# Block-diagonal HGRN states, alternating heads, and a smaller DMA scratch in the mixers of a two-block net

## The chip, the cores and the metric

The kernel runs on one core of a Trainium2 chip. Its time is the device time of one execution in microseconds; three executions of the kernel before gave 3905.02, 3905.59 and 3907.46 us. A core has TensorE (PE, the matrix engine, whose weight loads the profile counts apart as PEld), VectorE (DVE), ScalarE (ACT), GpSimd (POOL) and the DMA queues, each with its own stream of instructions, tied together by semaphores.

## The reference

A float32 net on 512 latent tokens and 256 context tokens of width 1024. Block 1 has two layers, each with token mixers and a mixture of 16 experts. Block 2 (differential attention, forgetting attention, two feed-forward nets) follows and isn't touched. The change is in the mixers of block 1: neighbourhood attention with six heads, HGRN2 with six heads, a short convolution. The HGRN2 part runs a gated linear recurrence over the tokens, once forward and once backward, context first; the context's last state starts the latents:

```python
def step(s, xs):                      # one chunk; s is a [64, 64] state per head
    qc, kc, gc, vc = xs
    a = jnp.cumsum(gc, axis=2)
    ...
    scores = jnp.sum(qc[:, :, :, None, :] * kc[:, :, None, :, :] * decay, axis=-1)
    o = jnp.einsum('bhts,bhsv->bhtv', scores, vc) + jnp.einsum('bhtk,bhkv->bhtv', qc * jnp.exp(a), s)
    a_last = a[:, :, -1:, :]
    s_new = jnp.exp(a_last[:, :, 0, :, None]) * s + jnp.einsum('bhsk,bhsv->bhkv', kc * jnp.exp(a_last - a), vc)
    return s_new, o
```

In the neighbourhood attention each query scores a window of 256 nearby latent keys and all 256 context keys, with one softmax over both.

## The kernel before

Activations lie with channels on the partitions and tokens on the free axis. Two heads of width 64 make a pair that fills 128 partitions; so there are three head pairs for HGRN and three for the neighbourhood attention. `mixers` runs, for each pair p: five columns of the input projection (`take`), `hgrn(p)`, three more columns, `na_prepare` and `na_attention`. A tile scheduler orders the instructions of each engine by priority when the program is built: projections are marked `later`, so they fill the places at which the mixers wait. HGRN has its own thread of PSUM banks, tag "s" (four); the attention uses tag "f" (two).

Projections. A weight tile is split on ScalarE into a rounded part (`wh`, line 244) and on VectorE into the rest (`wl`, line 245), three buffers of each. TensorE multiplies three times (lines 252 to 254).

Modulation in the background. Matrix-vector products run on VectorE (line 174). Their tiles `g` have two buffers and are loaded by DMAs that GpSimd issues (line 166), in order.

HGRN of one pair (`hgrn`, lines 715 to 766). The 768 tokens are six chunks of 128. `hg_gates` gives the decays' sums. `hg_sums` forms, for two chunks g at a time, the key-value sums: four transposes (line 784), eight matmuls in which the heads alternate (line 793), one copy of 128x256 out of PSUM (line 795). Eight steps on VectorE make states from the sums (line 739), in the tile `ls`, which `hg_gates` hands back as `kv`. A state is 128x64: rows 0 to 63 hold the first head's, rows 64 to 127 the second's. Then for each two chunks, `hg_scores` makes the scores `sc` on three engines, down to 32x32 products (line 821) and copies of 32x32 diagonals (line 835). At line 760 the output is added up in PSUM, head by head and chunk by chunk: score times value (`vt`, 128x64 weights), then state times query for each direction (64x64 weights). ScalarE copies it out (line 762). Last come the sums of squares of a head's output (line 479) and what VectorE makes of them (line 482). Layer 0 puts out all six chunks, layer 1 the four of the latents. Chunks 0 and 1 have one state product a head each, the others two.

Neighbourhood attention. `scores(j)` fills, for each of four query blocks j, one bank a head: 256 window scores (line 573) and 256 context scores (line 574). `values(j)` multiplies the transposed probabilities with the values, heads alternating (line 600), and ScalarE copies the result out (line 601).

Of the kernel before, what the change touches and what calls it, by code (L numbers as in the profile page):

```python
# [17 lines left out]
D, T, TC, KD = 1024, 512, 256, 8  # L18
TA = T + TC
CHUNKS = (8, 7, 7)  # L20
NEG = -1.0e30
KSTART = (0, 8, 24, 32)
# [29 lines left out]
class Slots:  # L52
    """A pool whose tags have their own numbers of buffers."""
# [8 lines left out]
class Net:  # L62
# [16 lines left out]
    @contextmanager  # L79
    def phase(self, name, sb, ps):  # L80
        """A part of the net with its own temporaries, in SBUF and in PSUM."""
        with self.tc.tile_pool(name=name, bufs=1, reuse_waits="tile") as s, self.psum(name, ps):
            old, self.tp = getattr(self, "tp", None), Slots(s, sb)
            yield
            self.tp = old
# [11 lines left out]
    def later(self, by=LATER):  # L97
        """What gives way to everything else that is ready."""
        return self.tc.high_priority(offset=-by)
# [5 lines left out]
    def on(self, psum, small):  # L105
        """A thread of its own: its banks and its small tiles."""
# [38 lines left out]
    def cond(self, name):  # L145
        """silu of a condition on every partition, and the generator that loads it."""
        cb = self.gp.tile([128, D], F32, tag="cb", name="cb", bufs=2)
        src = self.a[name]
# [9 lines left out]
    def gemv(self, wT, tiles, targets):  # L158
        """wT: [n, 128, 1024] in DRAM; targets: list of (cond tile, dst [128, n], bias).
        A generator: each step loads a tile and computes with the one before."""  # L160
# [24 lines left out]
    def paced(self, ins, wait=False):  # L185
        """Not issued before the last product so far, or not begun before its end."""
# [4 lines left out]
    def fill(self, n):  # L191
        """n steps of the matrix-vector products in the background."""
# [13 lines left out]
    def first_mods(self):  # L206
        """Shift and scale of the first norm, latent and context, on the tensor engine. A generator, a step for
        each block of the contraction."""
# [23 lines left out]
    def split(self, src, nk):  # L232
        """The rounded part and the rest of nk blocks [128, 128]."""
# [37 lines left out]
    def newton(self, y, v):  # L271
        """y = v ** -0.5."""
# [9 lines left out]
    def inv_rms(self, st, tag=None, paced=False):  # L282
        """1 / rms of each token, tokens on the partitions: [128, blocks]."""
# [14 lines left out]
    def spread(self, y, paced=False):  # L298
        """[128, blocks] to all partitions, tokens on the free axis."""
# [14 lines left out]
    def normed(self, x, r, A, B, split=True, pool=None, tag=None):  # L314
        """(x * rstd) * A + B, as its rounded part and the rest, or whole."""
# [30 lines left out]
    def transposed(self, dst, src, n, tag=None):  # L346
        """dst[:, j, :] = src[:, 128 j:128 (j + 1)]^T for n blocks."""
# [13 lines left out]
    def project(self, w, nf, h, evac, ks=range(KD), tags="m"):  # L361
        """w: [nf/2, 128, 2*1024] packed tiles; evac(f, psum). A generator, a step for each tile."""
# [19 lines left out]
    def lower_bounds(self):  # L382
        """For each direction and layer > 0: log lb, log(1 - lb), and their difference, per channel."""
# [18 lines left out]
    def mixers(self, l, h, hc):  # L402
        """Token mixers: the mixed tokens, 8 tiles for the latents and 8 for the context."""
# [65 lines left out]
    def head_rstd(self, segs, n, tag="nt"):  # L469
        """1 / rms over each 64 partitions, for tiles [128, tokens]; one PSUM tile each."""  # L470
# [25 lines left out]
    def na_prepare(self, l, p, d, need):  # L496
        """Normed and rotated queries and keys; values with the tokens on the partitions."""
# [57 lines left out]
    def na_attention(self, l, p, d, mix, mixc, need):  # L555
# [8 lines left out]
        def scores(j):  # L564
            v = (0, 1, 1, 2)[j]
            S = []
            for e in range(2):
                es = slice(64 * e, 64 * e + 64)
                if (e, v) not in bias:
                    bias[e, v] = self.na_bias(nb, e, v)  # L570
                b = self.bank()
                qb = q[es, 128 * j:128 * j + 128]
                nc.tensor.matmul(b[:, :256], qb, k[es, :, KSTART[j]:KSTART[j] + 32], start=True, stop=True)
                nc.tensor.matmul(b[:, 256:], qb, d["nk", "o"][es], start=True, stop=True)
                S.append(b)
# [96 lines left out]
    def hg_gates(self, l, p, S):  # L672
        """S: [first logits, -, -, second logits]. Over it, for the keys k and the decays' running sums c within
        each 128 tokens: [c1 - log k1, c1, c2, c2 + log k2]; c2 leaves out the token itself. Also the sums' ends,
        and k1 + k2."""
# [38 lines left out]
        return tot, ls[:, 0], ls[:, 1]  # L714

    def hgrn(self, l, p, d, mix, mixc, need):
        """The tokens lie context first; chunks of 128."""
        nc = self.nc
        S, q = d["z"], d["hq"]
        tot, ks, kv = self.hg_gates(l, p, S)  # L720
# [11 lines left out]
        kv = kv.rearrange("p (s c m) -> p s c m", s=2, c=6)  # L732
# [8 lines left out]
        for g in range(0 if need else 1, 3):  # L741
# [7 lines left out]
            for e in range(2):  # L749
                es = slice(64 * e, 64 * e + 64)  # L750
                first = True
                for i in range(2):
                    c, cs = 2 * g + i, slice(128 * i, 128 * i + 128)
                    ops = [(vt[:, c, es], sc[:, e, i])]
                    for dr in range(2):
                        if c != orders[dr][0]:
                            before = orders[dr][orders[dr].index(c) - 1]
                            ops.append((kv[es, dr, before], qt[es, dr, cs]))
                    for lhsT, rhs in ops:
# [942 lines left out]
```

## Time and profile before

| what | value |
| --- | --- |
| median of three executions | 3905.59 us |
| span of the profiled execution, first to last instruction | 3901.2 us |
| mean granted TensorE clock | 0.963 |
| TensorE busy | 3663.6 us, 94% |
| VectorE busy | 2172.9 us, 56% |
| ScalarE busy | 1445.6 us, 37% |
| GpSimd busy | 147.8 us, 4% |

The profiler gives the span from the first to the last instruction; the median of the timed executions lies 4.4 us above it. The mixers of layer 0 run from about 75 to 520 us, those of layer 1 from about 1040 to 1420 us. The experts come between and behind, block 2 from about 1800 us on. A float32 matmul leaves two records in the trace. In a row of a timeline "x4" means four such records in a run, the first number is where it starts and the second how long until the last ends; "[0.79 <-DVE sc L835]" is idle time of the engine just before, and what ended it. Names like `t` stand for the temporaries `t1` (queries with decay, `qt`), `s`, `f` and `m` for the banks.

### The profile page before, as it was taken

To read this page: it belongs to the slowest core of one execution; us is meant where nothing else is said; L and a number is where in the kernel's file an instruction comes from. 1 tells how busy PE (TensorE), PEld (TensorE's weight loads), DVE (VectorE), ACT (ScalarE), POOL (GpSimd) and SP (SyncE) were. 2 spreads that over 40 slices of the span, in tenths; PEclk is the share of its full clock that TensorE was granted. 3 is DMA by queue.
4 is the path that set the end of the run, shared out by engine and by line. 5 is a ranking of instruction groups with operands and counts; after the bars stand their busy time and mean duration, and the time that the engine had idled before them with its cause. 6 is when DMAs were issued, how large, how long until landed. Compare 5 with 4: busy or idle time off the path is not lost. (4 is left out here: it accounts for less than half of the span.)

```text
span 3901.2 us, 54964 instructions
## 1 busy us (share of the span) xinstructions
PE 3663.6 (94%) x21248; PEld 2659.1 (68%) x21248; DVE 2172.9 (56%) x5458; ACT 1445.6 (37%) x2827; POOL 147.8 (4%) x267
## 2 busy tenths in 40 slices
PE   7999998999899997988999998999989999999998
PEld 4777785333577775535888776788868888677887
DVE  5899874122688864215566665655643334764334
ACT  4566431111456631113233454323333233553222
POOL 0000000000000000000010000001100000000000
PEclk8999998999999997999999998999989999999999
DMA  5223254876433465995555321455522222012222
GB/s 203 70 80 101 77 196 167 327 275 259 156 111 109 135 215 199 356 356 179 194 194 189 113 76 54 142 193 205 191 80 97 96 94 95 33 52 79 97 102 81
DMA packets 154197, 588.04 MB, mean 151 GB/s; under 512 B 18048, under 2 KB 57256, under 8 KB 111952
## 3 DMA queue, kind: packets, MB, share of 16 engines
q1 hardware_dynamic: 113760, 442.43, 31.5%
q0 software_dynamic: 37872, 137.90, 10.5%
q10 hardware_dynamic: 2304, 4.20, 0.3%
q8 instruction: 167, 2.74, 0.3%
q14 instruction: 94, 0.77, 0.1%
HBM read 575.01 MB, written 9.46 MB: 150 GB/s over the span
## 5 line engine op out<-in xcount | busy, mean ns | idle before, releaser
L245 DVE TENSOR_TENSOR wl<-raw,wh 128x512 fp32r<-128x512 f32 (+1 forms) x826 | 558.3, 677 | 722.4 <-ACT wh L244 712.8
L244 ACT ACTIVATE wh<-raw 128x512 fp32r<-128x512 f32 (+1 forms) x826 | 512.1, 622 | 1203.2 <-PE m L253 835.1
L252 PE MATMUL m<-h,wh 128*128 128x512 f32 x1632 | 661.3, 406 | 30.6 <-DVE t L323 8.4
L253 PE MATMUL m<-h,wh 128*128 128x512 f32 x1632 | 658.3, 404 | 6.6 <-DVE h L326 5.2
L254 PE MATMUL m<-h,wl 128*128 128x512 f32 x1632 | 658.8, 404 | 1.1 <-DVE wl L245 1.1
L174 DVE SCALAR_TENSOR_TENSOR junk<-g,cb 128x512 bf16<-128x512 f32 (+1 forms) x440 | 374.1, 850 | 29.8 <-DMA g<-in_modT 17.5
L252 PEld LDWEIGHTS m<-h,wh 128*128 128x128 f32 x1632 | 315.4, 193 | 104.5 <-ACT h L325 19.1
L253 PEld LDWEIGHTS m<-h,wh 128*128 128x128 f32 x1632 | 313.8, 192 | 81.1 <-DVE h L326 16.3
L254 PEld LDWEIGHTS m<-h,wl 128*128 128x128 f32 x1632 | 313.9, 192 | 68.7 <-issue 6.9
L254 PE MATMUL m<-e,wl 128*128 128x512 f32 x832 | 325.7, 392 | 7.9 <-DVE wl L245 7.9
L252 PE MATMUL m<-e,wh 128*128 128x512 f32 x832 | 325.3, 391 | 0.5 <-ACT wh L244 0.5
L253 PE MATMUL m<-e,wh 128*128 128x512 f32 x832 | 324.9, 391 | 0.0
L252 PE MATMUL f<-h,wh 128*128 128x512 f32 x768 | 299.5, 390 | 0.0
L254 PE MATMUL f<-h,wl 128*128 128x512 f32 x768 | 299.1, 389 | 0.0
L253 PE MATMUL f<-h,wh 128*128 128x512 f32 x768 | 299.0, 389 | 0.0
L1106 PE MATMUL m<-raw,xg 128*64 128x512 f32 (+1 forms) x1264 | 258.5, 609 | 10.5 <-DMA raw<-in_exp_gu 10.5
L254 PEld LDWEIGHTS m<-e,wl 128*128 128x128 f32 x832 | 157.0, 189 | 40.9 <-DVE wl L245 8.3
L1106 PEld LDWEIGHTS m<-raw,xg 128*64 128x64 f32 (+1 forms) x1264 | 64.1, 126 | 175.0 <-issue 147.6
L252 PEld LDWEIGHTS m<-e,wh 128*128 128x128 f32 x832 | 157.2, 189 | 33.5 <-ACT wh L244 1.3
L253 PEld LDWEIGHTS m<-e,wh 128*128 128x128 f32 x832 | 157.0, 189 | 32.7
L252 PEld LDWEIGHTS f<-h,wh 128*128 128x128 f32 x768 | 144.5, 188 | 30.1 <-PE m L253 0.2
L254 PEld LDWEIGHTS f<-h,wl 128*128 128x128 f32 x768 | 144.3, 188 | 30.3 <-DVE wl L245 0.2
(455 smaller groups left out, 5170.0 us busy)
## 6 DMA issues: line engine op xcount, KB each, us to landing
raw<-in_exp_gu SPq DMA_DIRECT2D x98, 1024.0 KB, 6.6
raw<-in_ffn_in SPq DMA_DIRECT2D x88, 1024.0 KB, 4.8
g<-in_adaT POOLq DMA_DIRECT2D x144, 512.0 KB, 3.9
raw<-in_exp_dn SPq DMA_DIRECT2D x48, 1024.0 KB, 6.7
g<-in_modT POOLq DMA_DIRECT2D x80, 512.0 KB, 3.9
raw<-in_w_in SPq DMA_DIRECT2D x30, 1024.0 KB, 4.8
raw<-in_ffn_out SPq DMA_DIRECT2D x32, 896.0 KB, 4.6
raw<-in_ffn_out SPq DMA_DIRECT2D x16, 1024.0 KB, 4.7
```

Of the source, the lines that this page charges most:

```text
L174: self.paced(nc.vector.scalar_tensor_tensor(self.junk, before[0][:, js], 1.0, cb[:, js], op0=OP.mult, op1=OP.mult, accum_out=part[:, j:j + ...
L244: self.nc.scalar.activation(hi, src, AF.Copy)
L245: self.nc.vector.tensor_tensor(lo, src, hi.bitcast(F32), op=OP.subtract)
L252: nc.tensor.matmul(out, wh[k], hh[k], start=(first and k == ks[0]), stop=False)
L253: nc.tensor.matmul(out, wh[k], hl[k], start=False, stop=False)
L254: self.last = nc.tensor.matmul(out, wl[k], hh[k], start=False, stop=(last and k == ks[-1]))
L1106: self.nc.tensor.matmul(out[es, c:c + n], xg[:, es], t, start=start, stop=stop)
```

## The change

- In `scores(j)` both heads' banks are taken first; the order is window e0, window e1, context e0, context e1, where it was window e0, context e0, window e1, context e1.
- The states get a tile of their own, `kv`, 128 x 2 directions x 6 chunks x 128. Each state is a 128x128 block with the first head's 64x64 in one corner, the second's in the opposite one, and zeros elsewhere. GpSimd zeroes the tile in each call of `hgrn`; `hg_sums` copies out of PSUM in two parts of 64 partitions; the recurrence runs over 128x128.
- The output in `hgrn` adds first the states, one matmul of 128x128 weights for both heads, 54 where there were 108, and then the 60 products of score and value, heads alternating.
- The scratch for the descriptors of DMAs that GpSimd issues is 8192 bytes a partition; it was the default.

The other hunks remove docstrings and comments. The core of the diff:

```diff
@@ scores
-            S = []
+            S = [self.bank(), self.bank()]
             for e in range(2):
-                es = slice(64 * e, 64 * e + 64)
                 if (e, v) not in bias:
                     bias[e, v] = self.na_bias(nb, e, v)
-                b = self.bank()
-                qb = q[es, 128 * j:128 * j + 128]
-                nc.tensor.matmul(b[:, :256], qb, k[es, :, KSTART[j]:KSTART[j] + 32], start=True, stop=True)
-                nc.tensor.matmul(b[:, 256:], qb, d["nk", "o"][es], start=True, stop=True)
-                S.append(b)
+            for part in range(2):
+                for e in range(2):
+                    es = slice(64 * e, 64 * e + 64)
+                    ks = d["nk", "o"][es] if part else k[es, :, KSTART[j]:KSTART[j] + 32]
+                    nc.tensor.matmul(S[e][:, 256 * part:256 * part + 256], q[es, 128 * j:128 * j + 128], ks,
+                                     start=True, stop=True)
@@ hgrn
-        kv = kv.rearrange("p (s c m) -> p s c m", s=2, c=6)
+        kv = self.tmp("kv", 2 * TA).rearrange("p (s c m) -> p s c m", s=2, c=6)
+        nc.gpsimd.memset(kv, 0.0)
         for g in range(3):
             self.hg_sums(g, S, tot, vt, kv)
...
             po = self.bank()[:, :256]
-            for e in range(2):
-                es = slice(64 * e, 64 * e + 64)
-                first = True
-                for i in range(2):
-                    c, cs = 2 * g + i, slice(128 * i, 128 * i + 128)
-                    ops = [(vt[:, c, es], sc[:, e, i])]
-                    for dr in range(2):
-                        if c != orders[dr][0]:
-                            before = orders[dr][orders[dr].index(c) - 1]
-                            ops.append((kv[es, dr, before], qt[es, dr, cs]))
-                    for lhsT, rhs in ops:
-                        nc.tensor.matmul(po[es, cs], lhsT, rhs, start=first, stop=False, skip_group_check=True)
+            first = True
+            for i in range(2):
+                c, cs = 2 * g + i, slice(128 * i, 128 * i + 128)
+                for dr in range(2):
+                    if c != orders[dr][0]:
+                        before = orders[dr][orders[dr].index(c) - 1]
+                        nc.tensor.matmul(po[:, cs], kv[:, dr, before], qt[:, dr, cs], start=first, stop=False,
+                                         skip_group_check=True)
                         first = False
+            for i in range(2):
+                for e in range(2):
+                    es, cs = slice(64 * e, 64 * e + 64), slice(128 * i, 128 * i + 128)
+                    nc.tensor.matmul(po[es, cs], vt[:, 2 * g + i, es], sc[:, e, i], start=False, stop=False,
+                                     skip_group_check=True)
@@ hg_sums
-        nc.vector.tensor_copy(kv[:, :, 2 * g:2 * g + 2], pv[:, :256].rearrange("p (s c m) -> p s c m", s=2, c=2))
+        pv = pv[:, :256].rearrange("p (s c m) -> p s c m", s=2, c=2)
+        for e in range(2):
+            es = slice(64 * e, 64 * e + 64)
+            nc.vector.tensor_copy(kv[es, :, 2 * g:2 * g + 2, es], pv[es])
@@ kernel
-    nc = bacc.Bacc("TRN2", target_bir_lowering=False, num_devices=1)
+    nc = bacc.Bacc("TRN2", target_bir_lowering=False, num_devices=1, dynamic_dma_scratch_size=8192)
```

Where the program puts these instructions follows. Lines in the changed kernel are a few numbers higher: 756 is the state product, 762 score times value, 800 the two copies, 740 the recurrence, 733 the zeroing, 826 the scores' products.

TensorE before, the output of the second two chunks of the first head pair; `sc,hvt` is score times value, `t_1046,ls` state times query.

```order
L254 MATMUL m<-h,wl 128x512
L252 MATMUL m<-c,wh 128x256
L760 MATMUL s<-sc,hvt 64x128
L760 MATMUL s<-t_1046,ls 64x128 x2
L760 MATMUL s<-sc,hvt 64x128
L760 MATMUL s<-t_1046,ls 64x128 x2
...
L821 MATMUL s<-hx 128x128 x4
L821 MATMUL s<-hx 64x64 x8
```

Both kinds of product stand together, in turns, behind the finished scores.

TensorE of the change, the third two chunks of the same pair; `t_1225,kv` is state times query, `hx` and `hq,ls` are the scores' products, `halves` sums of squares.

```order
L826 MATMUL s<-hx 32x32 x16
L756 MATMUL s<-t_1225,kv 128x128 x4
L479 MATMUL f<-halves,nt 128x2 x4
L826 MATMUL s<-hx 32x32 x16
...
L826 MATMUL s<-hx 32x32 x16
L830 MATMUL s<-hq,ls 32x32 x16
...
L254 MATMUL m<-h,wl 128x512
L762 MATMUL s<-sc,hvt 64x128 x4
L252 MATMUL m<-c,wh 128x256
```

The state products have moved ahead, to where their operands are ready, among the scores' products; only four matmuls stand behind the finished scores. Between the two places there are 24 projection matmuls of 512 columns, 15 of 256, and four groups of 16 small products.

GpSimd before, from the start; `cb` are the conditions, `g` the modulation tiles, `row` the experts' gathers.

```order
L151 DMA cb<-in_c 128x1024
L151 DMA cb<-in_c_ctx 128x1024
L166 DMA g<-in_modT 128x1024 x48
L992 DMA row<-scratch_h,idx_6624 128x1024 x2
L992 DMA row<-scratch_c,idx_6997 128x1024
```

GpSimd of the change, the same stretch.

```order
L733 MEMSET kv 128x1536
L151 DMA cb<-in_c 128x1024
L151 DMA cb<-in_c_ctx 128x1024
L166 DMA g<-in_modT 128x1024 x6
L733 MEMSET kv 128x1536
L166 DMA g<-in_modT 128x1024 x11
L733 MEMSET kv 128x1536
L166 DMA g<-in_modT 128x1024 x31
```

Three zeroings of layer 0 now stand in the queue, two of them among the loads of modulation tiles; layer 1 has three more, the first ahead of its first load, the others 12 and 11 loads further on.

VectorE of the change, the place at which the tile behind the second zeroing is first read: `hsmall<-s` is the step on the sums of squares, and the read with DMASW0 in its waits is that tile's.

```order
L177 TENSOR_TENSOR mctx_83<-part 128x1 [waits DVE_49]
L482 TENSOR_SCALAR hsmall<-s 128x12 [waits PE_49]
L280 SCALAR_TENSOR_TENSOR small<-small 128x12 [waits DVE_49]
L174 SCALAR_TENSOR_TENSOR junk,part<-g,cb 128x512 [waits DMASW0_49]
L275 TENSOR_SCALAR hsmall<-hsmall 128x12 [waits DVE_49]
L488 COPY nt<-small 128x512 [waits DVE_49]
L278 TENSOR_TENSOR hsmall<-hsmall 128x12 [waits DVE_49]
L488 COPY nt<-small 128x256
L279 SCALAR_TENSOR_TENSOR hsmall<-hsmall 128x12 [waits DVE_49]
L245 TENSOR_TENSOR wl<-raw,wh 128x512 [waits DMAHW5_49,Activation_49]
```

Before, the read of the same tile stood seven rows ahead of the step; now it stands two rows behind it.

## Rows read from the trace of the kernel before

**Rows 1.** The page: busy time of TensorE, share of the span, instructions.

```profile
PE 3663.6 (94%) x21248; PEld 2659.1 (68%) x21248; DVE 2172.9 (56%) x5458; ACT 1445.6 (37%) x2827; POOL 147.8 (4%) x267
```

**Rows 2.** Busy times in both mixer stretches: the sum row (instructions left out).

```profile
sum 825.00, PE 779.43 PEld 604.54 DVE 697.84 ACT 463.13 POOL 51.45; mean PE 389.71 PEld 302.27 DVE 348.92 ACT 231.57 POOL 25.72
```

**Rows 3.** Waits of TensorE, 75 to 520: total us, times, longest.

```profile
PE s L760 <- DVE sc L835: 5.2, 7, 1.0
```

**Rows 4.** Waits of VectorE, 75 to 520, then 1040 to 1420.

```profile
DVE wl L245 <- ACT wh L244: 15.0, 7, 5.1
...
DVE junk L174 <- DMA g<-in_modT: 13.2, 6, 3.9
```

**Rows 5.** Line 760 in the whole trace: count, min/median/max ns, first, last, forms.

```profile
L760 PE MATMUL s<-t,ls x216: 269/269/472, 128.9 to 1363.3; 64*64 64x128 f32 x108
...
L760 PE MATMUL s<-sc,hvt x120: 272/294/475, 128.6 to 1362.7; 128*64 128x128 f32 x120
```

**Rows 6.** Timeline of TensorE, first output run: start, length, what, [idle before].

```profile
128.61 0.40 PE L760 MATMUL s<-sc,hvt 128*64 128x128 f32 x2 [0.79 <-DVE sc L835]
...
131.47 0.38 PE L821 MATMUL s<-hx 64*128 64x128 f32 x2
```

**Rows 7.** The same for the second output run.

```profile
147.77 0.43 PE L760 MATMUL s<-sc,hvt 128*64 128x128 f32 x2
148.13 0.65 PE L760 MATMUL s<-t,ls 64*64 64x128 f32 x4
148.71 0.43 PE L760 MATMUL s<-sc,hvt 128*64 128x128 f32 x2
```

**Rows 8.** The same for weight loads of the first run.

```profile
128.94 0.19 PEld L760 LDWEIGHTS s<-t,ls 64*64 64x64 f32 x2 [0.17 <-issue]
```

**Rows 9.** TensorE at the neighbourhood values of one block, then the next scores.

```profile
189.67 0.39 PE L253 MATMUL m<-h,wh 128*128 128x512 f32 x1
189.90 0.40 PE L254 MATMUL m<-h,wl 128*128 128x512 f32 x1
190.23 0.66 PE L600 MATMUL f<-nt,nv 128*64 128x128 f32 x8
190.72 0.61 PE L600 MATMUL f<-nt,nvc 128*64 128x128 f32 x8
191.25 0.93 PE L573 MATMUL f<-ev,nq 64*128 64x256 f32 x3
...
192.24 0.59 PE L574 MATMUL f<-evc,nq 64*128 64x256 f32 x2
```

**Rows 10.** TensorE at four transposes of the key factors, and what follows.

```profile
106.38 0.66 PE L784 MATMUL s<-ident,t 128*128 128x128 f32 x4
106.79 0.48 PE L252 MATMUL m<-h,wh 128*128 128x512 f32 x1
```

**Rows 11.** End of the first head pair: TensorE's last output products, VectorE's next step.

```profile
168.24 0.54 PE L760 MATMUL s<-t,ls 64*64 64x128 f32 x3
...
171.74 0.17 DVE L482 TENSOR_SCALAR hsmall<-s 128x12 f32<-128x12 f32 x1 [3.23 <-PE s L479]
```

**Rows 12.** TensorE at the scores of a first block.

```profile
176.80 0.71 PE L573 MATMUL f<-ev,nq 64*128 64x256 f32 x4
177.31 0.63 PE L574 MATMUL f<-evc,nq 64*128 64x256 f32 x4
```

**Rows 13.** VectorE by line and form, 75 to 1420: count | busy us, mean ns.

```profile
L811 DVE TENSOR_TENSOR hx<-hz 128x256 f32<-128x256 f32 x105 | 44.0, 420 | 19.5 <-PE s L821 19.3
...
L739 DVE SCALAR_TENSOR_TENSOR ls<-ls,hsmall 128x64 f32<-128x64 f32 x48 | 12.2, 278 | 0.0
...
L795 DVE COPY ls<-s 128x256 f32<-128x256 f32 x18 | 7.6, 423 | 4.4 <-PE s L793 3.9
```

**Rows 14.** The chain of waits in block 2: start, length, what.

```profile
2829.63 0.47 POOL g L166
...
2836.02 1.23 DVE junk L174 x2
```

More of the change, by code (lines that the diff above doesn't have):

```diff
@@ L713, in hg_gates @@
         nc.vector.tensor_add(ls[:, 0], ls[:, 0], ls[:, 1])
-        return tot, ls[:, 0], ls[:, 1]
+        return tot, ls[:, 0]
     def hgrn(self, l, p, d, mix, mixc, need):
@@ L719, in hgrn @@
         S, q = d["z"], d["hq"]
-        tot, ks, kv = self.hg_gates(l, p, S)
+        tot, ks = self.hg_gates(l, p, S)
         m = mix[3 + p] = self.ap.tile([128, T], F32, "x", "mix")
```

2 rows, old and new, of the table ada are left out of this document.

## The prediction

> **What bounds the kernel now.** I first read the busy times of the page. TensorE works in 94% of the span [rows 1], so time taken off it is worth most where no other engine is close behind. Then the busy times of the two stretches in which the mixers run, 75 to 520 and 1040 to 1420 us, 825 us together: TensorE 779, VectorE 698, ScalarE 463 [rows 2]. The reader is to see two things: TensorE is idle for only 825 − 779 = 46 us, and VectorE, with 127 us idle, is nearer to it here than in the whole span. Next the waits of both engines. TensorE hardly waits for VectorE: the largest such row is 5.2 us, for the scores' diagonal at the output product [rows 3]. VectorE waits for ScalarE's rounded weights, 15.0 us, and for modulation tiles, 13.2 us [rows 4]. ScalarE in its turn rounds into one of three buffers that TensorE empties, so this wait is TensorE's pace passed back. The mixers are TensorE's, with VectorE next.
>
> **The output product (state and values).** All records stand under one line: 216 of the state product, in 64x64 tiles, 120 of the value product, in 128x64 tiles [rows 5]; a float32 matmul leaves two records, so these are 108 and 60 matmuls. They come in 15 runs, one for each pair of chunks. In the three runs of the context chunks, of 16 records, the two forms alternate: 131.47 − 128.61 = 2.86 us [rows 6]. In the other twelve, of 24 records, a round of two value records, 0.36, and four state records, 0.58, takes 148.71 − 147.77 = 0.94 [rows 7], and four rounds 3.76. Together 3×2.86 + 12×3.76 = 53.7 us.
> The rows show why it is so long: the weight load of each new form starts after 0.17 us in which nothing holds it but issue [rows 8], and there are eight such changes in a run.
> After: each run has 8 value records, heads alternating. The neighbourhood values are that form already: 16 records in 191.25 − 190.23 = 1.02 us [rows 9], so 8 take 0.51, and with one change of form, 0.17, it is 0.68; 15×0.68 = 10.2 us.
> The 54 full-size state products have 108 records of 128x128 with 128 columns. The nearest rows are the four transposes, each with its own load, in 106.79 − 106.38 = 0.41 us [rows 10], 0.103 a record: 11.1 us. The order puts most of them beside projections, which are of the same form; some six runs stand between two groups of 32x32 products, as the run in the second order shown, or between these and sums of squares, and cost about two changes of 0.17 each, 2.0 us. Sum 10.2 + 11.1 + 2.0 = 23.3; TensorE saves 53.7 − 23.3 = 30 us. Bounds: if a full-size record takes the 0.18 us that a value record takes in rows 7, the states cost 19.4, and the saving is 22; with no extra changes of form it is 35. I take 30, since the transposes differ from the new matmul only in that one operand is an identity.
> A rule speaks against this part. The Trainium skill, "TensorE: Matmul & The Clock Gate", section on LDWEIGHTS and the part on what overlaps, gives a load P/1.2 ns (107 for 128 columns) and lets it overlap running matmuls only where their row groups differ. By it a full-size record is load plus stream, about 0.16 us as an estimate from that page, the states cost 17.3 instead of 11.1, and the saving is 24. The trace disagrees: four transposes of this size with four loads in 0.41 us [rows 10].
>
> **The wait before it.** The state products no longer stand behind the diagonal copies, so when these end only 0.5 us of work is left in front of ScalarE's copy, where 2.9 to 3.8 us were. In six places the wait for the last sums of squares, 3.23 us in the first pair [rows 11], may fall by up to 3 us. This is the same time as above seen from VectorE, and I don't count it again.
>
> **Neighbourhood scores.** The two heads already use different halves of the rows, and in a first block they run side by side: 176.80 to 177.94, 1.14 us [rows 12]. In a third block the second head starts late and the group takes 191.25 to 192.83, 1.58 us [rows 9]. Its bank is the one that the values of an earlier block left, and that is still so: when that bank comes free decides, not the order. I cost the interleaving at 0. Bounds: if all of some 14 late groups took 1.14, −14×0.44 = −6 us; if the first head now waits with the second's bank in each, +14×0.2 = +3.
>
> **VectorE.** The state's copy of 128x256 takes 423 ns, 18 times; the two copies that replace it cover half the partitions with as many elements a partition. If the time goes with the elements of a partition, +18×423 = 7.6 us; at the least 0. I take 7.6, as 128x256 on another line takes 420 [rows 13]. The recurrence grows from 128x64, 278 ns, to 128x128, which lies between that and the 420 of 256: near 0.34, 48×0.065 = 3.1 us (bounds 0 and 6.8). VectorE rises by 10.7 to 709 us of a stretch that should shorten to some 800.
>
> **GpSimd.** The zeroing has no row. VectorE's 420 ns for a sixth of its elements [rows 13] makes 2.5 us; the bounds are 0 and that, and I take 2, as the size is what counts. It is a wait more than a cost: GpSimd's queue is in order, the zeroing waits for the last state product of the pair before, and behind it stand the loads of the modulation tiles. The seventh, which before had nothing but a free buffer to wait for, now waits for that product. From GpSimd's start to the first read of a tile the chain shows 2836.02 − 2829.63 = 6.4 us [rows 14], so the tile can be read 8.4 us after the last state product. When is it wanted? The order puts the read two rows behind the sums-of-squares step. In the old run that step comes at 171.74, 3.5 us after the start of the last products of the output at 168.24 [rows 11]. And in the new order 24 projections of 512 columns stand between the last state product and the last value products, 0.23 us each [rows 9], 5.5 us, with 15 of 256 columns and four groups of small products besides, at least 8 us together. So the read is wanted 8 + 3.5 = 11.5 us after the product, and the tile is there by 8.4. In layer 1 the held tiles are read 11 and 5 rows behind the step, in the third pair 30. I take 0 for the standing; the bounds are 0 and six times 8, 48. The halved scratch of the descriptors costs nothing: at most two tile loads are in flight.
>
> **Sum.** TensorE −30. VectorE has 10.7 us more to do, on an engine busy for 709 of some 800; TensorE has only three buffers of split weights to outlast it, and the copies and the recurrence lie in the chain of each head pair. I charge it nearly whole, +10. Net −20 on the profiled span of 3901.2, so 3881; the runs' median is 4.4 above that span, and the forecast in its terms is 3905.6 − 20 = 3886 us. Its own range: saving 22 with 14.4 charged (both upper bounds of VectorE) and 3 for the scores, 3901; saving 35 with nothing charged, 3871.
>
> **Rivals.**
> Gain swallowed: VectorE at 709 of 800 sets the pace and TensorE's 30 us become waits for split weights. For it: VectorE's 85% in these stretches. Against: its largest wait is for ScalarE's weights, which TensorE's buffers hold back. With 4 us passed on, 3902: no change.
> The zeroing holds the queue (the slower side): one place, the tile loads behind the six memsets. If every held load comes 8 us after VectorE wants it, VectorE stands for 48 us, with the split of the next weights queued behind the read, and TensorE behind that; it decides from the point at which more than 30 us of it reach TensorE, and with all of it the time is 3905.6 − 30 + 48 = 3924. For it: the order shows the memsets ahead of the loads, and VectorE already waits 13.2 us for such tiles [rows 4]. Against: the distance worked out above.
> More than forecast: the shorter tail frees banks earlier, the late score groups run side by side, −6, and only 2 us of VectorE's work show: 3905.6 − 30 − 6 + 2 = 3872.
> That the change doesn't do what it says holds for the interleaving, which I price at 0.
>
> **How the numbers follow.** A difference under 0.2% (7.8 us) can't be told from none here. Forecast 0.65, swallowed gain 0.17, slower side 0.10, more than forecast 0.08. Of the forecast's case 0.02 lies within 0.2%. Faster 0.63 + 0.08 = 0.71, same 0.17 + 0.02 = 0.19, slower 0.10. The range reaches from 3870, below the best case, to 3903, past the swallowed gain's 3902; it leaves out the slower side, and part of the swallowed gain.
>
> **What would show it.** Right: 15 value runs of 8 records near 0.5 us; state records 0.10 to 0.12 apart beside projections; TensorE's busy time in the two stretches 25 to 35 us lower; VectorE's two copies near 420 ns each; no new VectorE wait for a modulation tile over 2 us behind a memset. Wrong: full-size state records at 0.16 us or more; TensorE's waits for split weights up by 15 us or more; waits for modulation tiles of 20 us or more in all.

## The result and the profile after

The changed kernel takes 3868.8 us in the median (four runs, 3863.0 to 3874.4) against 3906.5 (four runs); the ratio is 0.9898, 95% interval 0.9885 to 0.9911. That is 38 us less, where 20 were forecast, and just outside the range. The profiled span is 3864.0 us against 3901.2.

Where the time went is seen by cutting both traces at the same projection matmuls: from the first product of line 252 in the program to the 513th (mixers of layer 0), and from the 561st to the 961st (layer 1). Before, these stretches took 502.7 and 428.8 us; now 488.4 and 402.1, together 41.0 less. The rest of the span takes 2973.6 us, where it was 2969.7; in the profiles of the experiments below, none of which changes its instructions, it lies between 2966.8 and 2983.3. So the gain lies in the mixers, and layer 1, with six of the 15 output runs, gains more than layer 0 with nine.

The busy times of the changed kernel in the two stretches; the columns are length, then TensorE, its weight loads, VectorE, ScalarE, GpSimd, the granted clock, and the DMA share and rate.

```profile
40.96:529.32 488.36, 459.57 (x4547) 364.30 (x4547) 430.94 (x1339) 259.69 (x555) 28.25 (x50) 0.96 0.30 101
1032.79:1434.88 402.09, 381.75 (x3432) 298.39 (x3431) 334.45 (x1007) 237.69 (x467) 31.91 (x57) 0.98 0.46 156
sum 890.45, PE 841.31 PEld 662.69 DVE 765.39 ACT 497.38 POOL 60.16; mean PE 420.66 PEld 331.34 DVE 382.69 ACT 248.69 POOL 30.08
```

The same two stretches before, their sum:

```profile
sum 931.48, PE 875.43 PEld 683.59 DVE 755.92 ACT 497.90 POOL 54.69; mean PE 437.71 PEld 341.79 DVE 377.96 ACT 248.95 POOL 27.34
```

So TensorE's busy time fell by 34.1 us and its idle time from 56.1 to 49.1, though VectorE is now busy for 765 of 890 us, 86% (81% before).

The new products, by line in the whole trace; they answer to [rows 5].

```profile
L756 PE MATMUL s<-t,kv x108: 275/275/377, 118.8 to 1317.7; 128*128 128x128 f32 x108
...
L762 PE MATMUL s<-sc,hvt x120: 272/273/324, 129.6 to 1331.0; 128*64 128x128 f32 x120
```

The lengths of single records say little, because records overlap; their spacing counts. TensorE's timeline in the first run, which answers to [rows 6]:

```profile
118.56 0.35 PE L826 MATMUL s<-hx 64*32 64x32 f32 x32
118.84 0.71 PE L756 MATMUL s<-t,kv 128*128 128x128 f32 x4
119.48 0.35 PE L826 MATMUL s<-hx 64*32 64x32 f32 x32
...
129.60 0.66 PE L762 MATMUL s<-sc,hvt 128*64 128x128 f32 x8
130.19 0.88 PE L826 MATMUL s<-hx 64*128 64x128 f32 x18
```

Four state records take 0.64 us, eight value records 0.59, and the states are done 10 us before the values. Added up from the first record of each run to the next instruction, the 17 runs of states take 13.7 us and the 15 of values 8.8, 22.5 where the old runs took 54.4 in the same way. The wait in front of them, TensorE's waits for the scores' diagonal in both stretches (answering to [rows 3]):

```profile
PE s L762 <- DVE sc L840: 0.9, 2, 0.5
...
PE s L762 <- DVE sc L840: 0.8, 3, 0.3
```

Before, these were 5.2 and 4.1 us. VectorE's added work by form, 75 to 1381 us, and one of its waits (answering to [rows 13]):

```profile
L800 DVE COPY kv<-s 64x256 f32<-64x256 f32 x36 | 15.2, 422 | 4.1 <-PE s L795 3.5
...
L740 DVE SCALAR_TENSOR_TENSOR kv<-kv,hsmall 128x128 f32<-128x128 f32 x48 | 14.7, 347 | 0.2
...
L816 DVE TENSOR_TENSOR hx<-hz 128x256 f32<-128x256 f32 x105 | 44.1, 422 | 2.1 <-PE s L826 1.6
```

A copy of half the partitions takes 422 ns, as long as the whole one took; the wider recurrence takes 347 ns. VectorE's wait for TensorE's products of the scores, 19.3 us before at line 811, is 1.6 us. GpSimd's zeroing, and VectorE's step on the sums of squares at the end of the first pair (answering to [rows 11]):

```profile
L733 POOL MEMSET kv<- 128x1536 f32 x6 | 8.3, 1384 | 306.5 <-DVE c L326 238.6 <-PE f L219 34.3 <-PE s L756 33.6
```

```profile
165.78 0.17 DVE L482 TENSOR_SCALAR hsmall<-s 128x12 f32<-128x12 f32 x1 [1.09 <-PE s L479]
```

This wait was 3.23 us. Over all six places it fell from 15.5 to 7.5 us.

VectorE's waits for modulation tiles, 75 to 500 us and then layer 1 (answering to [rows 4]):

```profile
DVE junk L174 <- DMA g<-in_modT: 0.2, 1, 0.2
...
DVE junk L174 <- DMA g<-in_modT: 13.8, 5, 6.9
```

The first window ends before a wait of 4.5 us at the end of the layer-0 mixers. With it layer 0 has 4.7 us, where the kernel before has 4.3, 3.2 of them at the same place.

### A third term: the clock

The work doesn't explain why the stretches of most experiments below differ. Idle time and the granted clock do. At the end of the layer-1 mixers TensorE projects the mixed tokens and runs dry while VectorE finishes the last tiles. The kernel before, in pieces of 5 us (columns as above):

```profile
1415.00:1420.00 5.00, 3.89 (x16) 2.56 (x15) 5.00 (x11) 1.02 (x2) 0.00 (x0) 1.00 1.02 410
1420.00:1425.00 5.00, 2.29 (x5) 1.50 (x6) 3.69 (x12) 1.26 (x2) 0.53 (x1) 0.60 1.05 372
1425.00:1430.00 5.00, 5.00 (x21) 4.69 (x20) 1.40 (x4) 0.63 (x1) 0.00 (x0) 0.50 1.02 420
1430.00:1435.00 5.00, 3.70 (x15) 2.96 (x14) 2.44 (x7) 0.77 (x2) 0.00 (x0) 0.50 0.64 222
```

TensorE stands for 3.07 us, and the clock goes from 1.00 to 0.50, that is from 2.4 to 1.2 GHz, and stays there for more than 10 us. The Trainium skill, "TensorE: Matmul & The Clock Gate", "What's actually happening", says that idleness throttles the array to half the clock and that activity releases it. The trace agrees with the first half, with the four rows above; of the release they show nothing, as in the third TensorE is busy for all 5 us and the clock stays at 0.50.

The changed kernel at the same work, and its one dip near by, behind a wait of 1.48 us:

```profile
1370.00:1375.00 5.00, 4.87 (x30) 3.49 (x31) 4.82 (x14) 2.37 (x7) 0.48 (x1) 0.66 0.99 365
...
1385.00:1390.00 5.00, 5.00 (x32) 3.54 (x31) 3.75 (x8) 4.03 (x8) 0.46 (x1) 1.00 0.47 143
1390.00:1395.00 5.00, 5.00 (x30) 4.40 (x30) 4.62 (x16) 1.27 (x2) 0.00 (x0) 1.00 0.81 243
```

A stop doesn't always cost as much. Earlier in layer 1 the changed kernel stands for 4.22 us, and its clock is back at 1.00 in the third of these pieces:

```profile
1269.06:1273.93 4.87, 0.71 (x6) 0.51 (x5) 4.83 (x10) 4.84 (x6) 0.00 (x0) 1.00 0.00 0
1273.93:1278.80 4.87, 4.80 (x17) 3.79 (x18) 2.74 (x5) 3.79 (x6) 0.53 (x1) 0.65 0.32 111
1278.80:1283.66 4.86, 4.86 (x23) 3.98 (x22) 4.86 (x15) 4.70 (x6) 0.53 (x1) 1.00 0.37 108
```

No run here isolates what decides between the two.

So I split the length of both stretches in three: TensorE's idle time; what the clock takes of its busy time (half of the busy time that falls where the granted clock is 0.50); and what is left, TensorE's work at full clock. The half is an approximation: the spacing of the same projections, shown further down, is 0.43 us against 0.23. The kernels in the table are those of the next section. Each row is one profile, up to 6.6 us from its kernel's median; the three profiles of the changed kernel differ by 0.5 us in work, 0.9 in idle time and 1.9 in the clock.

| kernel | ratio (interval) | length | idle | clock | work |
| --- | --- | --- | --- | --- | --- |
| before | 1 | 931.5 | 56.1 | 28.5 | 846.9 |
| changed | 0.9898 (0.9885–0.9911) | 890.4 | 49.1 | 22.2 | 819.1 |
| again | 0.9896 (0.9881–0.9911) | 891.0 | 48.2 | 24.1 | 818.7 |
| again2 | 0.9895 (0.9879–0.9910) | 890.7 | 49.1 | 22.4 | 819.2 |
| heads64 | 0.9899 (0.9884–0.9913) | 891.4 | 43.0 | 20.5 | 827.9 |
| heads64_scores | 0.9909 (0.9896–0.9923) | 897.1 | 44.4 | 28.7 | 824.0 |
| scores_only | 0.9993 (0.9981–1.0006) | 929.3 | 54.0 | 30.4 | 844.9 |
| scores_old | 0.9921 (0.9909–0.9934) | 899.3 | 49.9 | 24.7 | 824.7 |
| behind | 0.9928 (0.9915–0.9941) | 900.8 | 57.2 | 23.7 | 819.9 |
| zero_once | 0.9882 (0.9867–0.9897) | 885.6 | 46.8 | 19.8 | 819.0 |
| zero_once2 | 0.9898 (0.9883–0.9913) | 886.9 | 48.0 | 19.6 | 819.2 |
| gemv_pad | 0.9920 (0.9906–0.9934) | 903.2 | 54.3 | 27.1 | 821.9 |
| copies_twice | 0.9969 (0.9958–0.9980) | 920.4 | 66.2 | 28.5 | 825.8 |
| copies_split | 0.9947 (0.9933–0.9960) | 913.3 | 57.5 | 31.5 | 824.3 |
| copies_act | 0.9933 (0.9920–0.9947) | 908.3 | 53.3 | 36.2 | 818.8 |
| query_order | 0.9925 (0.9911–0.9938) | 895.4 | 49.9 | 25.8 | 819.8 |
| sums_order | 0.9939 (0.9925–0.9952) | 903.2 | 51.6 | 27.8 | 823.8 |

The change: work −28, idle −7, clock −6. Every kernel with the block-diagonal states and the interleaved scores stays between 819 and 826 us of work; they differ more in idle time and clock, which go from 67 us to 95 us together.

### The profile page after: what moved, and what is told of

The parts are those of the page before. It is cut to its first block, busy times and chain, and to the rows that moved or that the text cites. A ratio compares the mean times of both kernels' runs of the same rounds, so it can differ in the third digit from the quotient of the medians.

```text
span 3864.0 us, 54771 instructions
## 1 busy us (share of the span) xinstructions
PE 3628.6 (94%) x21140; PEld 2640.8 (68%) x21140; DVE 2182.7 (56%) x5476; ACT 1444.8 (37%) x2826; POOL 156.0 (4%) x273
```

## The experiments

**again, again2.** The changed kernel, unchanged.

> The changed kernel unchanged, once more beside the others. Expected by both theories: ratio 0.990 as measured (0.9885 to 0.9911).

> The changed kernel unchanged, as the measure for the three others on this chip: 0.990, within 0.0015.

0.9896 and 0.9895. The gain holds.

**behind.** Both kinds of product behind the scores, values first.

```diff
-            first = True
+            for i in range(2):
+                for e in range(2):
+                    es, cs = slice(64 * e, 64 * e + 64), slice(128 * i, 128 * i + 128)
+                    nc.tensor.matmul(po[es, cs], vt[:, 2 * g + i, es], sc[:, e, i], start=i == 0, stop=False,
+                                     skip_group_check=True)
             for i in range(2):
...
-                        nc.tensor.matmul(po[:, cs], kv[:, dr, before], qt[:, dr, cs], start=first, stop=False,
+                        nc.tensor.matmul(po[:, cs], kv[:, dr, before], qt[:, dr, cs], start=False, stop=False,
                                          skip_group_check=True)
-            for i in range(2):
-                for e in range(2):
...
```

> The changed kernel with the order in the output product turned round: score times value first, the full-size state products behind it, so that both wait for the finished scores as before. Theory (about 30 us from TensorE's work, the rest from waiting that the earlier state products cover): TensorE's time in the two products 22 to 25 us as in the changed kernel, the wait for the scores' diagonal back at about 9 us, ratio 0.9925 (3877). Rival one (only the work counts): 0.990. Rival two (standing ahead of the scores is most of it): 0.996 or more.

Its waits for the diagonal, layer 0 and layer 1:

```profile
PE s L753 <- DVE sc L838: 5.8, 7, 1.1
...
PE s L753 <- DVE sc L838: 3.1, 4, 1.1
```

0.9928: the wait is back, 8.9 us where the changed kernel has 1.7, at the same work (819.9). As the theory said. The wait is 7 us of the 12 by which the ratios differ; the other 5 may come from the order of other instructions. So the earlier place of the states is worth 7 to 12 us, their form the larger part.

**heads64.** Of the kernel before, only the output's order changes; the heads stay in 64x64 tiles, in turns.

```diff
...
+            first = [True, True]
+            for i in range(2):
...
+                        for e in range(2):
+                            es = slice(64 * e, 64 * e + 64)
+                            nc.tensor.matmul(po[es, cs], kv[es, dr, before], qt[es, dr, cs], start=first[e], stop=False,
+                                             skip_group_check=True)
+                            first[e] = False
+            for i in range(2):
+                for e in range(2):
+                    es, cs = slice(64 * e, 64 * e + 64), slice(128 * i, 128 * i + 128)
+                    nc.tensor.matmul(po[es, cs], vt[:, 2 * g + i, es], sc[:, e, i], start=False, stop=False,
+                                     skip_group_check=True)
```

> The kernel before with only the order of the output product changed: all state products first, in 64x64 tiles of one head as before but with the two heads in turns, then score times value with the heads in turns. No block-diagonal tile, no zeroing, one copy out of PSUM, recurrence over 128x64, scratch and neighbourhood scores as before. Theory (the order is what counts): the 216 state records run side by side by heads, about 0.064 us each as the neighbourhood values do, 13.8 us, the same as the full-size form's 13.7 in the changed kernel's trace; ratio 0.990. Rival (the full-size block is needed): 0.107 us a record as before, 23 us, so 9 us less gained: 0.9925 or worse.

Its state products, one run of them, and its two stretches:

```profile
L757 PE MATMUL s<-t,ls x216: 269/269/321, 117.6 to 1316.3; 64*64 64x128 f32 x108
```

```profile
131.87 1.09 PE L757 MATMUL s<-t,ls 64*64 64x128 f32 x16
132.89 0.38 PE L254 MATMUL m<-c,wl 128*128 128x256 f32 x1
```

```profile
40.01:526.46 486.45, 463.74 (x4606) 364.71 (x4607) 424.72 (x1331) 261.26 (x557) 25.48 (x48) 0.97 0.30 102
1033.13:1438.13 405.00, 384.68 (x3480) 299.38 (x3479) 328.91 (x998) 238.11 (x467) 29.22 (x55) 0.98 0.45 154
```

0.9899, the whole gain without the block-diagonal tile. Its 216 records take 15.8 us added up as above, 0.073 each, and 0.064 in the run shown; the full-size form takes 13.7. TensorE works 9 us more than in the changed kernel, 2 of them in the state products, and stands for 6 us less, with 12 us less on VectorE. So what counts is that equal forms stand together, with the heads in turns, and that the states stand early; how the gain divides between these in the 64x64 form no run shows. The block, half of which is zeros, makes the state products 2 us shorter, and the whole kernel no faster.

**scores_old, scores_only, heads64_scores.** The order of the neighbourhood scores, taken back in the changed kernel, put alone into the one before, and put into heads64 (the diff is the one of the change, the other way round in the first).

> The changed kernel with the scores of the neighbourhood attention in the order of before (window and context of one head, then of the other); all else as changed. Theory (the whole gain is TensorE's time and TensorE's waiting at the HGRN output product): as the changed kernel, ratio to before 0.990, within 0.0015. Rival (the interleaved scores brought the 17 us by which the forecast fell short): 0.9945.

> The kernel before with the interleaved neighbourhood scores alone. Forecast: no change, between -6 and +3 us, ratio 0.9985 to 1.0008. Rival (the interleaving is worth 9 us): 0.9977.

> The kernel before with the output product's new order in 64x64 tiles (heads in turns, no block-diagonal tile, no zeroing, no added work on VectorE) and the interleaved neighbourhood scores. Theory one (the interleaving is worth the 9 us by which the changed kernel beats the one without it): 9 us less than the 64x64 form without it, ratio 0.9875. Theory two (those 9 us came from another order of the whole program): 0.990, within 0.0015.

0.9921, 0.9993, 0.9909. In all three pairs the interleaved form has less work, by 5.6, 2.0 and 3.9 us; in the second and third the clock takes about as much or more (+1.9 and +8.2). But the products of the neighbourhood scores themselves, at full clock and from each record to the next, take 36.2 us in the changed kernel against 38.5 in scores_old, 36.0 in scores_only against 36.3 before, and 37.7 against 37.9 in the third pair. So only 2.3, 0.3 and 0.2 us lie in them, and the rest in other products, which stand in another order. Alone the interleaving can't be told from no change, as forecast. Taken out of the changed kernel it costs 9 us, against the theory that I held; that this is the interleaving, and not another order of the whole, isn't shown (orders with no such change cost 11 and 16 us, below). The rival's reading, a fixed 9 us, fails in the other two.

**copies_twice, copies_split, copies_act, gemv_pad.** What VectorE's work costs: the copies doubled, split by direction, moved to ScalarE; and as much work outside the chain of the head pairs.

The doubled copies:

```diff
-            nc.vector.tensor_copy(kv[es, :, 2 * g:2 * g + 2, es], pv[es])
+            for _ in range(2):
+                nc.vector.tensor_copy(kv[es, :, 2 * g:2 * g + 2, es], pv[es])
```

The split copies:

```diff
-        for e in range(2):
-            es = slice(64 * e, 64 * e + 64)
-            nc.vector.tensor_copy(kv[es, :, 2 * g:2 * g + 2, es], pv[es])
+        for dr in range(2):
+            for e in range(2):
+                es = slice(64 * e, 64 * e + 64)
+                nc.vector.tensor_copy(kv[es, dr, 2 * g:2 * g + 2, es], pv[es, dr])
```

The copies on ScalarE:

```diff
-            nc.vector.tensor_copy(kv[es, :, 2 * g:2 * g + 2, es], pv[es])
+            nc.scalar.activation(kv[es, :, 2 * g:2 * g + 2, es], pv[es], AF.Copy)
```

The padding, at every sixth product of a modulation tile in the mixers:

```diff
+                    self.nth = getattr(self, "nth", 0) + 1
+                    if getattr(self, "inmix", False) and self.nth % 6 == 0:
+                        spare = self.sp.tile([128, 2], F32, tag="part", name="part", bufs=4)
+                        self.paced(nc.vector.scalar_tensor_tensor(self.junk, before[0][:, :w], 1.0, cb[:, :w], op0=OP.mult,
+                                                                  op1=OP.mult, accum_out=spare[:, 0:1]))
...
+        self.inmix = True
         for p in range(3):
...
+        self.inmix = False
```

> The changed kernel with each of the 36 copies of the states out of PSUM made twice, which adds 36 x 0.42 = 15.2 us to VectorE in the chain of the head pairs, more than the change itself added (10.7). Theory (VectorE's added work is hidden behind TensorE's projections): 0 to 3 us more than the changed kernel, ratio 0.990 to 0.991. Rival (the charge that the forecast made, 10 us for 10.7): 14 us more, 0.9935.

> The changed kernel with 22 more passes of the background's matrix-vector product over 128x512, into a spare sum that nothing reads, spread over both mixer stages: 22 x 0.69 = 15 us more on VectorE, as much as the doubled copies of the states, but in no chain of a head pair. Theory one (VectorE has room; the doubled copies cost 27 us because they stand between the key-value sums and the states): 0 to 5 us, ratio 0.990 to 0.991. Theory two (VectorE's load itself is charged, wherever it stands): 15 to 27 us, ratio 0.9935 to 0.9969.

> The changed kernel with each state copy split by direction: 72 copies of 64x128 in place of 36 of 64x256, about 72 x 0.28 - 36 x 0.42 = 5 us more on VectorE in the chain of the head pairs, a third of what the doubled copies added. Theory one (time in that chain is charged): a third of 27, 9 us, ratio 0.992. Theory two (what the doubled copies cost came from another order of the program): no such proportion, anything between 0.989 and 0.997.

> The changed kernel with the 36 copies of the states out of PSUM on ScalarE in place of VectorE: 15.2 us less on VectorE, about as much more on ScalarE. Making these copies twice cost 27 us. Theory one (VectorE's added work reaches the end about one for one): 10 to 15 us less than the changed kernel, ratio 0.9865. Theory two (in the changed kernel VectorE's work is hidden; the second copies were dear only because they lengthened the chain or shuffled the order): within 4 us of it, ratio 0.990.

The two stretches with the copies doubled:

```profile
41.10:539.66 498.56, 464.62 (x4546) 366.24 (x4547) 441.41 (x1367) 256.77 (x553) 28.93 (x51) 0.95 0.30 100
1043.16:1465.03 421.87, 389.64 (x3433) 302.21 (x3432) 341.77 (x1025) 236.30 (x467) 32.05 (x57) 0.97 0.44 149
```

copies_twice 0.9969, gemv_pad 0.9920, copies_split 0.9947, copies_act 0.9933. My theory, that all this is hidden, falls. But no price per microsecond of VectorE fits either. In the two stretches its busy time rises by 18 us in copies_twice, which cost 28, by 14 in gemv_pad, which cost 9, and by 6 in copies_split, which cost 19; and 12 us taken off VectorE and put on ScalarE cost 14. To the stretches of the changed kernel, in the sequence of the ratios above, 30.0, 12.8, 22.9 and 17.9 us are added, and idle time and clock grow by 23.4, 10.1, 17.7 and 18.2.

**sums_order, query_order.** The same instructions in another order, no work added.

```diff
-        for g in range(3):
+        for g in (1, 0, 2):
             self.hg_sums(g, S, tot, vt, kv)
```

```diff
+            sc = self.hg_scores(g, q, S, ks)
             qt = self.tmp("t1").rearrange("p (s t) -> p s t", s=2)
             nc.scalar.activation(qt[:, 0], S[:, 1, sl], AF.Exp)
             self.hg_rest(qt[:, 1], tot[:, 1], S[:, 2], g)
             nc.vector.tensor_tensor(qt, qt, q[:, sl].unsqueeze(1).to_broadcast([128, 2, 256]), op=OP.mult)
-            sc = self.hg_scores(g, q, S, ks)
```

> The changed kernel with the key-value sums formed for the chunk pairs in the order 1, 0, 2 in place of 0, 1, 2: the same instructions with the same lengths on every engine, in another order over much of the mixers. Theory one (another order alone moves the time by as much as the splits of the copies did): somewhere between 0.988 and 0.997, apart from the changed kernel by 0.002 or more. Theory two (only added work or a longer chain moves it): 0.990, within 0.0015.

> The changed kernel with the decayed queries made after the scores in the program's text in place of before them: the same instructions with the same lengths, in another order over part of the mixers; the state products' operand comes later. Theory one (order alone moves the time): apart from the changed kernel by 0.002 or more. Theory two: 0.990, within 0.0015.

0.9939 and 0.9925: order alone costs 16 and 11 us (17 and 8 by the medians, 3883.4 and 3874.6, beside again2's 3866.6). In sums_order the end of the layer-1 mixers is this, first by pieces, then TensorE's timeline:

```profile
1390.00:1395.00 5.00, 3.82 (x15) 2.12 (x13) 5.00 (x11) 0.66 (x2) 0.53 (x1) 1.00 0.88 265
1395.00:1400.00 5.00, 0.08 (x1) 0.00 (x0) 4.29 (x13) 0.63 (x1) 0.53 (x1) 0.72 1.01 338
1400.00:1405.00 5.00, 4.85 (x15) 3.86 (x16) 0.89 (x3) 1.26 (x2) 0.00 (x0) 0.50 1.02 410
1405.00:1410.00 5.00, 4.04 (x16) 3.22 (x16) 3.84 (x11) 0.63 (x1) 0.00 (x0) 0.50 0.29 68
```

```profile
1394.68 0.40 PE L254 MATMUL m<-h,wl 128*128 128x512 f32 x1
1400.00 0.80 PE L252 MATMUL m<-h,wh 128*128 128x512 f32 x1 [4.92 <-ACT h L244]
...
1401.96 0.63 PE L252 MATMUL m<-h,wh 128*128 128x512 f32 x1
1402.39 0.63 PE L253 MATMUL m<-h,wh 128*128 128x512 f32 x1
```

The reader is to see VectorE at 4.29 of 5 us while TensorE has 0.08; then the clock at 0.50, where a projection takes 0.43 us (1402.39 − 1401.96) and not 0.23 [rows 9]. It is the place that the kernel before stumbles at, and the changed kernel in its own order does not.

**zero_once, zero_once2.** One tile of states for each mixer stage, zeroed once.

```diff
+        self.states = self.tp.pool.tile([128, 2 * TA], F32, name="kv").rearrange("p (s c m) -> p s c m", s=2, c=6)
+        self.nc.gpsimd.memset(self.states, 0.0)
         for p in range(3):
...
-        kv = self.tmp("kv", 2 * TA).rearrange("p (s c m) -> p s c m", s=2, c=6)
-        nc.gpsimd.memset(kv, 0.0)
+        kv = self.states
```

> The changed kernel with one tile of states for each mixer stage, zeroed once in it in place of three times: no zeroing is left among the loads of the modulation tiles but the first of each layer. Theory (the zeroings cost nothing): ratio 0.990, within 0.002. Rival (they hold GpSimd's queue): up to 14 us less, the longest wait for a tile behind one being 6.9 us and two such waits gone, 0.9865.

> The kernel with the states zeroed once in each mixer stage, again: by the first run 0.9882, 6 us below the changed kernel. If that was chance of the runs: 0.990; if the held tile loads cost it: 0.9885 or less, and waits of VectorE for modulation tiles lower by 5 us or more than in the changed kernel.

0.9882, then 0.9898. Its mixers are 4.8 and 3.5 us shorter than the changed kernel's in the two profiles, and VectorE's waits for modulation tiles in layer 1 are 8.8 and 7.9 us, where they were 13.8. But the ratios don't show it apart from the changed kernel: not settled, and no version beats the changed kernel clearly.

**scratch_only.** `dynamic_dma_scratch_size=8192` in the kernel before.

> The kernel before with the descriptors' scratch of 8192 bytes a partition alone; its instructions stand in the same order on every engine. Forecast and theory: no change, ratio 1.000 within 0.0015. Rival (the descriptors of the modulation tiles' loads crowd the smaller scratch, or come out faster): 0.997 or 1.003.

1.000 (0.9989 to 1.0010): no difference.

## Why the prediction missed, point by point

- TensorE's work at the output product, −30: it measured −31.9. The values took 8.8 us (10.2 forecast), the states 13.7 (11.1 + 2.0). This term was right in its sum, and so was the choice of the transposes as the nearest row.
- The wait in front. The step "This is the same time as above seen from VectorE, and I don't count it again" failed. The 53.7 us were counted from the first record of each run, so the 5.2 us of [rows 3], and 4.1 more in layer 1, stood ahead of them as idle time of TensorE's own. It fell from 9.3 to 1.8 us: −7.5. The run behind shows it from the other side. VectorE's wait for the sums of squares is another wait, and it fell too, from 15.5 to 7.5 us.
- VectorE. The added work has the size forecast (422 and 347 ns), but "I charge it nearly whole, +10" failed. TensorE's idle time away from the output product went from 46.8 to 47.3 us, so that here the work cost 0.5 us net. The charge left out that VectorE's own waits shrink: 19.3 us before for the scores' products [rows 13] became 1.6, and those for the sums of squares fell by 8, more than the 9.5 us by which its busy time rose. That the work went into this room is argued from the rows and not shown by a run. In heads64 and heads64_scores, with 12 us less on VectorE, TensorE's idle time is 6.1 and 4.7 us lower than in the changed kernel, so in idle time about half of the charge may be real; their ratios (0.9899, 0.9909) show no gain.
- These two steps make 17 of the 18 us that were missing. On the span, −37.2 is −31.9, −7.5 and +0.5 as above, −2.2 of TensorE's busy time away from the output product, and +3.9 in the rest of the program, which is within its spread. The clock had no place in the forecast. It gave back 6.3 us in the mixers: 5.4 at the end of layer 1, where the changed kernel does not run dry, and 2.7 earlier in that layer, less 1.8 in layer 0. But 1.0 of this lies in the output product, and other products took 3.1 us more at full clock, 2.5 of it the products of the HGRN scores (line 826), among which the states now stand; so only the 2.2 are left.
- The interleaved scores at 0: alone, 0.9993, right; their products take 36.2 us where they took 36.3. With the rest the order around them moved the time by some 9 us, which the bounds of −6 and +3 don't reach.
- GpSimd: 1.38 us a zeroing (2 taken), and no wait of VectorE behind the held tiles in layer 0, as worked out. The fourth zeroing stands ahead of the first loads of layer 1, and VectorE waits 6.9 us there, where the kernel before waited 3.3 and heads64, which zeroes nothing, 5.3; I had placed no cost at it, and zero_once leaves open whether it has one.
- Scratch: nothing, right.
- Of the rivals, "more than forecast" came true in its size (3872), and by half of the way that it named: the charge for VectorE was not due, but in place of the late score groups it was the wait that vanished. What the range lacked is the order: kernels with the same instructions lie 16 us apart.

## What to carry to other kernels

Count a wait in front of a group of instructions apart from the group; moving the group's independent part ahead shortened both here. Put matmuls of one tile form together and let the heads take turns: that, with the states ahead of the scores, gave the whole gain here, without the block-diagonal form. Before work is charged to a second engine, look at that engine's own waits, which the change may shorten, and at the end of the stage, where its backlog meets an empty TensorE. Stops of 3.1 and 4.9 us there were followed by losses of 7.0 and 6.6 us through the clock, and a small change of order decided whether they happened.

## What was not expected of the hardware

At the end of the layer-1 mixers a stop of TensorE of 3.1 us, in another order 4.9, was followed by more than 10 us at half its clock, in which the projections' spacing went from 0.23 to 0.43 us; behind a stop of 4.2 us elsewhere the half clock lasted less than 5 us. Products of 64x64 tiles with the heads in turns took 0.073 us a record, where in the old order the same records took 0.145 (0.58 us for four). A PSUM copy over 64 partitions took as long as one over 128 with the same elements a partition (422 and 423 ns).
